# Second layer's experts: outputs added to rows on the chip by one-hot products instead of scatters to memory

## The chip, the cores and the metric

The kernel runs on one core of a Trainium2 chip. A core has a matrix engine (TensorE, in the profile PE, its weight loads PEld), three engines for elementwise work (VectorE = DVE, ScalarE = ACT, GpSimd = POOL), a queue engine (SyncE = SP) and 16 DMA engines that all queues share. The metric is the device time of one execution in microseconds (us); lower is better.

## The reference, cut to what matters

Two blocks of two layers each are computed in float32. The change concerns the last step of the second block's second layer: 16 experts, each of which takes the 64 tokens (of 512) that it rates highest. Every expert's output is scaled by its rating, added into the rows of its tokens, scaled by a gate `m_lat[5]`, and added to the residual `x`. A row can be chosen by several experts or by none.

```python
vals, idx = lax.top_k(aff.transpose(0, 2, 1), cap)          # cap = 64
xg = jax.vmap(lambda hb, ib: hb[ib])(h, idx)
hid = silu(einsum('becd,edf->becf', xg, w_gate)) * einsum('becd,edf->becf', xg, w_up)
out = einsum('becf,efd->becd', hid, w_down) * vals[..., None]
moe = zeros((t, d)).at[ib.reshape(-1)].add(ob.reshape(-1, d))
x = x + m_lat[5] * moe
```

## The kernel before, in words

`block2` runs two layers. In each, `mixer2` does projections and attention and ends with the residual `x` in SBUF, features on partitions; `ffn` then does routing and experts. The first layer (`need` is true) also has a second stream of 256 context rows, and its sums are read back by `reload`; the second layer has only the 512 rows, and its sums are the kernel's output. `self.acc[0]` is a DRAM tensor in the first layer and the output tensor itself in the second.

Routing (`route`, lines 1537 to 1620) computes the ratings, turns `x` back to rows (line 1575) and writes each row block twice to DRAM through GpSimd's queue: normalized to `normed` (line 1578, from a tile `row`) and raw to `acc` (line 1579, from a tile `in`), where it is the start value of the sums. Then it takes the top 64 of each expert by eight rounds on VectorE (lines 1583 to 1589) and lays token numbers and ratings out as `gi` (128 rows of a pair of experts in one column, for gathers), `si` (for scatters) and `vw` (ratings), and the gate over all partitions.

Experts run in eight pairs q (`experts`, lines 1684 to 1783), 64 rows of each expert side by side on 128 partitions. For a pair, `fetch` gathers 128 rows from `normed` on GpSimd's queue, `inputs` transposes them (line 1678) and modulates them, `gate_up` multiplies with two weight matrices (line 1741), `hidden` makes the activations and transposes them (line 1715), `down` multiplies with the third matrix in two halves of 512 columns (line 1768) and scales by rating and gate (line 1771). Then `scatter` issues two indirect DMAs with addition, one per expert, 64 rows of 4 KB each (line 1788). The order is gate_up(0), gate_up(1), down(0), gate_up(2), down(1), ..., gate_up(7), down(6), down(7). The planner of the framework takes this text order as a priority and may put an instruction that it thinks ready ahead of an earlier one on the same engine; at run time each engine keeps that fixed order.

Weights come in 96 pieces of 1 MB through SP's queue (line 1640), twelve per pair. Each piece goes into one of 14 buffers in turn: 11 tiles `ew` and three that reuse the room of `x` and `cx`. A piece's transfer is issued when its buffer is free. The products of rows with weights are float32 with 64 columns of weights per expert, two experts next to each other in the array (TensorE runs each as two instructions); the projections of the layers before use F32R operands split into a rounded part and the rest (lines 472 to 474).

PSUM has banks by name: `g` and `s` two each, `t` two, `o` and `a` one each; in the second layer's experts `o` and `a` are not used.

Of the kernel before, what the change touches and what calls it, by code (L numbers as in the profile page):

```python
# [20 lines left out]
P = 128  # L21
D = 1024
# [26 lines left out]
def _bc(v):  # L49
    return np.ascontiguousarray(np.broadcast_to(v.reshape(1, -1), (P, v.size)))  # L50
# [40 lines left out]
def _layout(inp):  # L91
# [15 lines left out]
    vec, vec2, c2 = {}, {}, {}  # L107
    _layout2(g, A, vec2, c2)
    c2["id"] = np.eye(P, dtype=np.float32)
    A["const1"], coff = _pack(c)  # L110
    A["const2"], coff2 = _pack(c2)
    for l in range(DEPTH):
# [122 lines left out]
class _K:  # L235
# [1301 lines left out]
    def route(self, l, v, x, nt, cap, state, got):  # L1537
# [30 lines left out]
        wk = self.tl("y", [16, 512])[:, :W]  # L1568
        yield
        for i in range(nt):  # L1570
            raw, row = self.tl("in", [P, D]), self.tl("row", [P, D])
            for s in range(2):
                pq = self.pt("s")
                for k in range(4):
                    ten.transpose(pq[:, k * P:(k + 1) * P], x[:, 4 * s + k, i * P:(i + 1) * P], self.idf)
                act.activation(row[:, s * 512:(s + 1) * 512], pq, AF.Copy, scale=rs[:, i:i + 1])
                act.activation(raw[:, s * 512:(s + 1) * 512], pq, AF.Copy)
            nc.gpsimd.dma_start(self.normed[v][i * P:(i + 1) * P, :], row)
            nc.gpsimd.dma_start(self.acc[v][i * P:(i + 1) * P, :], raw)

        val = self.s1(f"val{v}", [16, cap])
        idx = self.s1(f"idx{v}", [16, cap], U32)
# [25 lines left out]
        vec.tensor_copy(si, pg[:cap, 16:32])  # L1608
        vw = self.s1(f"vw{v}", [P, 8])
        vec.tensor_copy(vw, pg[:, 8:16])  # L1610
        yield

        gate = self.s1(f"gate{v}", [P, D])
# [5 lines left out]
            act.activation(gate[:, s * 512:(s + 1) * 512], pq, AF.Copy)  # L1619
        got[v] = gi, si, vw, gate  # L1620

    def ffn(self, l, x, cx, need, states):
        nc, A = self.nc, self.A
        ten, vec, act = nc.tensor, nc.vector, nc.scalar
        acts = [("gu", 0)] + [a for q in range(1, 8) for a in (("gu", q), ("d", q - 1))] + [("d", 7)]
        pieces = []
        for what, q in acts:
            ee = (2 * q, 2 * q + 1)
            if what == "gu":
                pieces += [A[f"{n}{l}"][2 * e + j] for j in range(2) for n in ("eg", "eu") for e in ee]  # L1630
            else:
                pieces += [A[f"ed{l}"][2 * e + j] for j in range(2) for e in ee]

        spare = [x[:, :4], x[:, 4:], cx.rearrange("p (k h) c -> p k (h c)", h=2)]
        loaded = []

        def fetch():
            n = len(loaded) % (EW + len(spare))
            raw = self.tl("ew", [P, 4, 512]) if n < EW else spare[n - EW]
            nc.sync.dma_start(raw, pieces[len(loaded)].rearrange("p (k c) -> p k c", k=4))  # L1640
            loaded.append(raw)

        nxt = [0]

        def eload():
            if nxt[0] == len(loaded):
                fetch()
            nxt[0] += 1
            return loaded[nxt[0] - 1]

        for _ in range(EW):
            fetch()
        streams = [(0, x, 4, 64)] + ([(1, cx, 2, 32)] if need else [])
        got = {}
        run = [self.route(l, v, xs, nt, cap, states[v], got) for v, xs, nt, cap in streams]
        for _ in range(6):
            for r in run:
                next(r, None)
        self.experts(l, acts, got, eload)
        if need:  # L1660
            self.reload(x, cx)
# [22 lines left out]
    def experts(self, l, acts, got, eload):  # L1684
# [2 lines left out]
        nc = self.nc  # L1687
        ten, vec, act, pool = nc.tensor, nc.vector, nc.scalar, nc.gpsimd
        self.mods = {v: self.mod_cols(l, v, 3, self.v(f"n2{l}")) for v in got}
        two = 1 in got  # L1690
        rows, xg, hid = {}, {}, {}

        def fetch(q):
# [26 lines left out]
        def gate_up(q):  # L1720
# [3 lines left out]
            for j in range(2):  # L1724
# [12 lines left out]
                for ps, wn in ((pg, w[0]), (pu, w[1])):  # L1737
                    for k in range(4):
                        d = 4 * j + k
                        for e in range(2):  # L1740
                            ten.matmul(ps[e * 64:(e + 1) * 64], x0[:, d, e * 64:(e + 1) * 64], wn[e][:, k],  # L1741
                                       start=d == 0, stop=d == 7)
            hidden(q, 0, pg, pu, P)

        def down(q):
# [14 lines left out]
                    vec.scalar_tensor_tensor(y[:64, c], ps[r], val[r, q:q + 1], gate[r, c], OP.mult, OP.mult)  # L1760
                self.scatter(1, y, si, q, 32)
            gi, si, val, gate = got[0]
            y = self.tl("row", [P, D])
            for j in range(2):
                ps = self.pt("s")
                for f in range(4):
                    for e in range(2):
                        ten.matmul(ps[e * 64:(e + 1) * 64], hid[0, q][:, f, e * 64:(e + 1) * 64], w[j][e][:, f],  # L1768
                                   start=f == 0, stop=f == 3)
                c = slice(j * 512, (j + 1) * 512)  # L1770
                vec.scalar_tensor_tensor(y[:, c], ps, val[:, q:q + 1], gate[:, c], OP.mult, OP.mult)
            self.scatter(0, y, si, q, 64)

        fetch(0)
        fetch(1)
        inputs(0)
        for what, q in acts:
# [3 lines left out]
                gate_up(q)  # L1781
            else:
                down(q)

    def scatter(self, v, y, si, q, n):

# [24 lines left out]
    def block2(self, x, cx, rb, dram, out):  # L1811
        self.rs2 = self.one("rs2", [P, 6])
        for l in range(DEPTH):
# [2 lines left out]
                states = self.mixer2(l, x, cx, need, *rb)  # L1816
            self.normed = [dram.tile([n, D], F32, name=f"normed{l}{n}", tag=f"n{n}") for n in ((T, 256) if need else (T,))]
            self.acc = [dram.tile([n, D], F32, name=f"acc{l}{n}", tag=f"a{n}") for n in (T, 256)] if need else [out]
            with self.scope(ew=EW, row=4, **{"in": 4}, xg=4, hid0=2, **({"hid1": 2} if need else {}), t=5, sm=2, s1=1):
                self.ffn(l, x, cx, need, states)  # L1820
            rb = None, self.rs2


# [45 lines left out]
```

## Time and profile before

| what | value |
|---|---|
| median of 3 runs | 3001.3 us (3000.87 to 3002.17) |
| the profiled execution's own time | 3005.11 us |
| its span, first to last instruction | 3003.3 us |
| PE busy | 2790.8 us (93%) |
| DVE, ACT, POOL busy | 52%, 40%, 9% |
| mean granted TensorE clock | 0.972 |
| HBM read, written | 416.40 MB, 20.97 MB |
| GB/s in the last four fortieths of the span | 358, 408, 408, 296 |

Averages over the span say little here: the second layer's experts are the last 260 us, in which the DMA engines are at 400 GB/s and more, while the rest of the span is mostly TensorE. A prediction has to be read from that stretch. Lines of the trace carry the source line (L1768), the engine, the operation, and the tiles as out<-in.

### The profile page before, as it was taken

How to read it: one execution, taken by the hardware profiler on the slowest of the kernel's cores; microseconds unless marked ns; L12 is line 12 of the kernel's file. 1: busy time of each engine (PE TensorE's matmuls, PEld its weight loads, DVE VectorE, ACT ScalarE, POOL GpSimd, SP SyncE). 2: the span in 40 equal slices, each digit the busy share in tenths (PEclk: the TensorE clock that was granted, in tenths of full speed). 3: DMA queues.
4: the chain of work that ended last, by engine and by line, in shares of the span. 5: the costliest groups of instructions: out<-in, count | busy, mean ns of one | idle time of the engine just before them, and what ended most of it. 6: DMA issues, size and time to landing. Idle time of an engine off the chain costs nothing. (4 is left out here: it accounts for less than half of the span.)

```text
span 3003.3 us, 46941 instructions
## 1 busy us (share of the span) xinstructions
PE 2790.8 (93%) x19056; PEld 1938.7 (65%) x19056; DVE 1548.1 (52%) x3135; ACT 1198.9 (40%) x2468; POOL 279.7 (9%) x276
## 2 busy tenths in 40 slices
PE   7999999999999999998999999899996999997875
PEld 5677767977677767877776877633324767773321
DVE  4645786545555786645456556711115365574100
ACT  5545354443545354444455243331113363433110
POOL 0000031000000030000011011011111010001101
PEclk9999999999999999998999999999997999998998
DMA  4132425412232434521110111689974111129997
GB/s 141 56 134 92 169 99 175 156 57 79 67 121 92 153 107 142 168 85 52 43 39 22 58 44 30 254 338 373 366 271 132 51 34 56 52 77 358 408 408 296
DMA packets 97576, 439.55 MB, mean 146 GB/s; under 512 B 11216, under 2 KB 12496, under 8 KB 72784
## 3 DMA queue, kind: packets, MB, share of 16 engines
q1 hardware_dynamic: 86976, 401.09, 36.5%
q0 software_dynamic: 9520, 32.32, 4.0%
q8 instruction: 150, 2.46, 0.3%
q10 hardware_dynamic: 864, 3.15, 0.3%
q14 instruction: 66, 0.54, 0.1%
HBM read 416.40 MB, written 20.97 MB: 146 GB/s over the span
## 5 line engine op out<-in xcount | busy, mean ns | idle before, releaser
L472 PE MATMUL psg<-h,wh 128*128 128x512 f32 x1616 | 655.8, 407 | 6.7 <-ACT h L444 4.3
L473 PE MATMUL psg<-h,wh 128*128 128x512 f32 x1616 | 651.3, 403 | 0.0
L474 PE MATMUL psg<-h,wl 128*128 128x512 f32 x1616 | 647.2, 401 | 0.0
L462 DVE TENSOR_TENSOR wl<-wr,wh 128x1024 fp32r<-128x1024 f32 (+2 forms) x272 | 340.1, 1251 | 367.4 <-ACT wh L460 361.4
L460 ACT ACTIVATE wh<-wr 128x1024 fp32r<-128x1024 f32 (+2 forms) x272 | 280.5, 1032 | 470.7 <-PE psg L473 398.1
L472 PEld LDWEIGHTS psg<-h,wh 128*128 128x128 f32 x1616 | 307.5, 190 | 90.1 <-issue 18.5
L473 PEld LDWEIGHTS psg<-h,wh 128*128 128x128 f32 x1616 | 307.9, 191 | 68.6 <-issue 9.7
L474 PEld LDWEIGHTS psg<-h,wl 128*128 128x128 f32 x1616 | 307.2, 190 | 67.8 <-issue 6.0
L1741 PE MATMUL psg<-ew,xg 128*64 128x512 f32 x832 | 223.0, 609 | 22.6 <-DMA ew<-in_eu_dram 11.6
L472 PE MATMUL psg<-y,wh 128*128 128x256 f32 (+1 forms) x560 | 182.2, 326 | 1.5 <-ACT y L448 0.8
L473 PE MATMUL psg<-y,wh 128*128 128x256 f32 (+1 forms) x560 | 180.5, 323 | 1.9 <-DVE y L449 1.9
L474 PE MATMUL psg<-y,wl 128*128 128x256 f32 (+1 forms) x560 | 179.7, 322 | 0.2 <-DVE wl L462 0.2
L1741 PEld LDWEIGHTS psg<-ew,xg 128*64 128x64 f32 x832 | 65.4, 139 | 154.9 <-issue 113.6
L472 PE MATMUL psg<-f,wh 128*128 128x256 f32 (+1 forms) x360 | 113.3, 316 | 7.1 <-DVE x L582 4.9
L472 PEld LDWEIGHTS psg<-y,wh 128*128 128x128 f32 x560 | 108.4, 194 | 15.4 <-issue 2.1
L473 PEld LDWEIGHTS psg<-y,wh 128*128 128x128 f32 x560 | 108.2, 194 | 11.3 <-DVE y L449 2.2
L473 PE MATMUL psg<-f,wh 128*128 128x256 f32 (+1 forms) x360 | 113.0, 314 | 0.8 <-DVE f L1256 0.8
L474 PE MATMUL psg<-f,wl 128*128 128x256 f32 (+1 forms) x360 | 112.4, 312 | 0.6 <-DVE wl L462 0.5
L474 PEld LDWEIGHTS psg<-y,wl 128*128 128x128 f32 x560 | 108.6, 195 | 6.4 <-DVE wl L462 0.5
L1021 ACT ACTIVATE t<-pst 128x512 f32<-128x512 f32 (+1 forms) x134 | 69.4, 556 | 106.4 <-PE pst L1018 106.4
L1768 PE MATMUL pss<-ew,hid 128*64 128x512 f32 x400 | 106.4, 598 | 4.8 <-DMA ew<-in_ed_dram 4.7
L1018 PE MATMUL pst<-const_sb,t 128*128 128x128 f32 x488 | 83.4, 282 | 5.2 <-DVE t L1246 3.5
(484 smaller groups left out, 4583.0 us busy)
## 6 DMA issues: line engine op xcount, KB each, us to landing
ew<-in_eg_dram SPq DMA_DIRECT2D x52, 1024.0 KB, 10.9
ew<-in_eu_dram SPq DMA_DIRECT2D x52, 1024.0 KB, 20.4
ew<-in_ed_dram SPq DMA_DIRECT2D x50, 1024.0 KB, 10.4
wm<-in_wm_dram SPq DMA_DIRECT2D x96, 512.0 KB, 4.3
wr<-in_w_f_dram SPq DMA_DIRECT2D x92, 512.0 KB, 3.5
wr<-in_v_f_dram SPq DMA_DIRECT2D x60, 512.0 KB, 3.2
wr<-in_w_o_dram SPq DMA_DIRECT2D x32, 512.0 KB, 3.5
x<-in_ed_dram SPq DMA_DIRECT2D x10, 1024.0 KB, 16.0
```

The lines of the kernel that those rows point to most:

```text
L460: nc.scalar.activation(hi, raw, AF.Copy)
L462: nc.vector.tensor_tensor(lo, raw, hi, OP.subtract)
L472: t.matmul(ps, a[0], b[0], start=first, stop=False)
L473: t.matmul(ps, a[0], b[1], start=False, stop=False)
L474: t.matmul(ps, a[1], b[0], start=False, stop=last)
L1018: ten.transpose(pp[:, (2 * i + a) * P:(2 * i + a + 1) * P], ps[a][:, c:c + P], self.idf)
L1021: self.nc.scalar.activation(pT[:, :w], pp[:, :w], AF.Copy)
L1741: ten.matmul(ps[e * 64:(e + 1) * 64], x0[:, d, e * 64:(e + 1) * 64], wn[e][:, k], start=d == 0, stop=d == 7)
L1768: ten.matmul(ps[e * 64:(e + 1) * 64], hid[0, q][:, f, e * 64:(e + 1) * 64], w[j][e][:, f], start=f == 0, stop=f == 3)
```

## The change

In the second layer only, the raw rows stay in SBUF as four tiles `sum`, 128 rows of 1024 values each. For every pair a one-hot tile `oh` is made (128 chosen rows by 512 tokens: 1 where the token's number is the row's slot). The scaled output of each half is split into a rounded part (ScalarE) and the rest (VectorE), and for each of the four row blocks two F32R products (rounded part, rest) with a 128x128 slice of `oh` put the rows in their places in a PSUM bank, `o` or `a` in turn; VectorE adds the bank to the tile `sum`. A pair has two halves, four blocks and two products each: 16 products and 8 additions. They are a generator, `add`; the `gate_up` that follows in the order above (after down(0) that of pair 2) takes a step of it, two blocks, after each quarter of a weight piece, and the next `down` takes what is left. For the last pair the finished blocks are written to the output from SP's and ScalarE's queues. The raw rows are no longer written at the start and nothing is scattered. To make room, the layer has 10 tiles `ew` instead of 11, 3 each of `row`, `in` and `xg` instead of 4. A constant `iota` (numbers 0 to 511) is loaded on ScalarE's queue.

```diff
@@ route
-            raw, row = self.tl("in", [P, D]), self.tl("row", [P, D])
+            raw, row = self.tl("in" if self.two else "sum", [P, D]), self.tl("row", [P, D])
...
-            nc.gpsimd.dma_start(self.acc[v][i * P:(i + 1) * P, :], raw)
+            if self.two:
+                nc.gpsimd.dma_start(self.acc[v][i * P:(i + 1) * P, :], raw)
+            else:
+                self.total.append(raw)
...
+        if not self.two:
+            self.slot = self.s1("slot", [P, 8])
+            vec.tensor_copy(self.slot, pg[:, :8])
@@ ffn
-            n = len(loaded) % (EW + len(spare))
-            raw = self.tl("ew", [P, 4, 512]) if n < EW else spare[n - EW]
+            n = len(loaded) % (ew + len(spare))
+            raw = self.tl("ew", [P, 4, 512]) if n < ew else spare[n - ew]
...
+        self.two, self.total = need, []
@@ experts, gate_up
                             ten.matmul(ps[e * 64:(e + 1) * 64], x0[:, d, e * 64:(e + 1) * 64], wn[e][:, k],
                                        start=d == 0, stop=d == 7)
+                    next(spread[0], None)
@@ experts, down
-            y = self.tl("row", [P, D])
+            if two:
+                y = self.tl("row", [P, D])
+            else:
+                for _ in spread[0]:
+                    pass
+                oh = self.tl("oh", [P, 512], F32R)
+                vec.tensor_scalar(oh, io, self.slot[:, q:q + 1], None, OP.is_equal)
+                parts = []
...
-                vec.scalar_tensor_tensor(y[:, c], ps, val[:, q:q + 1], gate[:, c], OP.mult, OP.mult)
-            self.scatter(0, y, si, q, 64)
+                yc = y[:, c] if two else self.tl("t", [P, 512])
+                vec.scalar_tensor_tensor(yc, ps, val[:, q:q + 1], gate[:, c], OP.mult, OP.mult)
+                if not two:
+                    hi, lo = self.tl("yh", [P, 512], F32R), self.tl("yl", [P, 512], F32R)
+                    act.activation(hi, yc, AF.Copy)
+                    vec.tensor_tensor(lo, yc, hi, OP.subtract)
+                    parts.append((hi, lo))
+            if two:
+                self.scatter(0, y, si, q, 64)
+            else:
+                spread[0] = add(q, oh, parts)
+
+        def add(q, oh, parts):
+            for j, y in enumerate(parts):
+                c = slice(j * 512, (j + 1) * 512)
+                for i in range(4):
+                    ps = self.pt("oa"[i % 2])
+                    for n in range(2):
+                        ten.matmul(ps, oh[:, i * P:(i + 1) * P], y[n], start=n == 0, stop=n == 1)
+                    o = self.total[i][:, c]
+                    vec.tensor_tensor(o, o, ps, OP.add)
+                    if q == 7:
+                        (nc.sync, nc.scalar)[i % 2].dma_start(self.acc[0][i * P:(i + 1) * P, c], o)
+                    if i % 2:
+                        yield
+
+        spread = [iter(())]
+        if not two:
+            io = self.tl("y", [P, 512])
+            nc.scalar.dma_start(io, self.A["iota"])
...
+        for _ in spread[0]:
+            pass
@@ block2
-            with self.scope(ew=EW, row=4, **{"in": 4}, xg=4, hid0=2, **({"hid1": 2} if need else {}), t=5, sm=2, s1=1):
+            ew = EW if need else EW - 1
+            more = {"row": 4, "in": 4, "hid1": 2} if need else {"row": 3, "in": 3, "sum": 4, "oh": 1, "yh": 2, "yl": 2}
+            with self.scope(ew=ew, xg=4 if need else 3, hid0=2, **more, t=5, sm=2, s1=1):
```

## Rows read from the trace of the kernel before

**Rows 1.** Busy time by stretch: length, each engine's busy us, PEclk, DMA share, GB/s.

```profile
2742.00:2757.00 15.00, 11.39 (x52) 6.23 (x54) 0.31 (x3) 7.10 (x18) 5.75 (x6) 0.65 0.55 182
2757.00:2822.00 65.00, 62.52 (x298) 22.22 (x296) 7.12 (x10) 12.17 (x30) 6.25 (x5) 1.00 1.00 406
2822.00:2982.00 160.00, 123.84 (x524) 40.18 (x518) 15.13 (x21) 14.34 (x34) 14.03 (x10) 0.98 1.01 404
```

**Rows 2.** Order of time, SP's queue, weight pieces: start, us, engine, line, transfer.

```profile
2756.51 1.17 SPq L1640 DMA_DIRECT2D ew<-in_eu_dram  x2
...
2811.41 0.33 SPq L1640 DMA_DIRECT2D x<-in_eu_dram  x1
2813.90 0.33 SPq L1640 DMA_DIRECT2D x<-in_ed_dram  x1
```

**Rows 3.** DMA queues from 2757 to 2982: packets, MB, share of 16 engines.

```profile
q1 hardware_dynamic: 11808, 85.99, 91.3%
q0 software_dynamic: 1460, 4.96, 9.6%
```

**Rows 4.** Order of time at the end: last products, last scatter.

```profile
2982.30 0.64 PE L1768 MATMUL pss<-x,hid 128*64 128x512 f32 x1 [1.53 <-DMA x<-in_ed_dram]
...
2984.92 1.02 PE L1768 MATMUL pss<-x,hid 128*64 128x512 f32 x2
...
2993.62 1.41 POOL L1788 DMA_INDIRECT out_dram<-row,si  x1 [3.36 <-DMA out_dram<-row,si]
```

**Rows 5.** The closing line's drains: ns min/median/max, first and last start.

```profile
L1864 POOLq DRAIN  x3: 46/102/9153, 2993.4 to 3003.1; - x3
L1864 SPq DRAIN  x3: 7/7/7, 2998.6 to 3002.8; - x3
```

**Rows 6.** Order of time, F32R products of a projection and a weight load.

```profile
2699.10 0.40 PE L474 MATMUL psg<-h,wl 128*128 128x512 f32 x1
2699.10 0.19 PEld L472 LDWEIGHTS psg<-h,wh 128*128 128x128 f32 x1
2699.33 0.40 PE L472 MATMUL psg<-h,wh 128*128 128x512 f32 x1
```

**Rows 7.** Order of time on TensorE, 2753 to 2818, pairs 0 to 2.

```profile
2753.79 1.08 PE L1741 MATMUL psg<-ew,xg 128*64 128x512 f32 x4
...
2783.59 0.59 PE L1768 MATMUL pss<-ew,hid 128*64 128x512 f32 x1
2785.04 0.63 PE L1715 MATMUL pst<-const_sb,t 128*128 128x128 f32 x4 [0.86 <-DVE t L1712]
2785.60 7.08 PE L1768 MATMUL pss<-ew,hid 128*64 128x512 f32 x30
...
2793.64 7.51 PE L1741 MATMUL psg<-ew,xg 128*64 128x512 f32 x33
...
2816.95 0.59 PE L1768 MATMUL pss<-ew,hid 128*64 128x512 f32 x1
```

**Rows 8.** Groups by form: count, busy us, mean ns, idle before, releaser.

```profile
L1771 DVE SCALAR_TENSOR_TENSOR row<-pss,vw,gate 128x512 f32<-128x512 f32 x16 | 12.0, 751 | 67.9 <-PE pss L1768 67.9
...
L545 DVE TENSOR_TENSOR h<-f,h 128x512 fp32r<-128x512 f32 x1 | 0.7, 682 | 0.0
...
L544 ACT ACTIVATE h<-f 128x512 fp32r<-128x512 f32 x1 | 0.6, 633 | 0.8 <-DVE f L1504 0.8
```

**Rows 9.** DMA issues from 2640 to 2694: count, KB, median us to landing.

```profile
wr<-in_v_o_dram SPq DMA_DIRECT2D x4, 256.0 KB, 2.7
```

**Rows 10.** Line 1578, the writes of normed: landing.

```profile
DMA to landing us min/median/max: 5.4/8.7/12.0
```

**Rows 11.** Order of time in routing: write of normed, fourth row, first gather.

```profile
2723.32 0.62 POOL L1578 DMA_DIRECT2D normed<-row  x1 [58.63 <-ACT row L1576]
...
2728.36 0.72 ACT L1576 ACTIVATE row<-pss,rq_y 128x512 f32<-128x512 f32 x1
...
2743.76 1.02 POOL L1666 DMA_INDIRECT in<-normed,gi  x1 [12.09 <-DVE vw L1610]
```

More of the change, by code (lines that the diff above doesn't have):

```diff
@@ L109, in _layout @@
     c2["id"] = np.eye(P, dtype=np.float32)
+    A["iota"] = _bc(np.arange(T, dtype=np.float32))
     A["const1"], coff = _pack(c)
@@ L1620, in route, with ffn @@
         got[v] = gi, si, vw, gate
-    def ffn(self, l, x, cx, need, states):
+    def ffn(self, l, x, cx, need, states, ew):
         nc, A = self.nc, self.A
@@ L1649, in eload @@
             return loaded[nxt[0] - 1]
-        for _ in range(EW):
+        for _ in range(ew):
             fetch()
         streams = [(0, x, 4, 64)] + ([(1, cx, 2, 32)] if need else [])
+        self.two, self.total = need, []
         got = {}
@@ L1689, in experts @@
         self.mods = {v: self.mod_cols(l, v, 3, self.v(f"n2{l}")) for v in got}
-        two = 1 in got
+        two = self.two
         rows, xg, hid = {}, {}, {}
@@ L1818, in block2 @@
             self.acc = [dram.tile([n, D], F32, name=f"acc{l}{n}", tag=f"a{n}") for n in (T, 256)] if need else [out]
-            with self.scope(ew=EW, row=4, **{"in": 4}, xg=4, hid0=2, **({"hid1": 2} if need else {}), t=5, sm=2, s1=1):
-                self.ffn(l, x, cx, need, states)
+            ew = EW if need else EW - 1
+            more = {"row": 4, "in": 4, "hid1": 2} if need else {"row": 3, "in": 3, "sum": 4, "oh": 1, "yh": 2, "yl": 2}
+            with self.scope(ew=ew, xg=4 if need else 3, hid0=2, **more, t=5, sm=2, s1=1):
+                self.ffn(l, x, cx, need, states, ew)
             rb = None, self.rs2
```

## The prediction

> **What bounds the kernel now.** I read in this order: busy time by stretch for the end of the kernel, where layer 2's experts run; then the order of issue on SP's queue; then the table of DMA queues; then TensorE's order of time; last the end. By stretch [rows 1], the weight prefetch has stopped between 2742 and 2757 (DMA share 0.55: every weight buffer is full until the first products free one), and from 2757 to 2982 the 16 DMA engines are busy without a gap (share 1.00 to 1.01, 404 to 406 GB/s), while TensorE has idle time only after 2822. So the stage is bounded by TensorE at first, working off what was prefetched, and by the weight stream afterwards. The reader should see on SP's queue that undisturbed 1 MB pieces are issued 2.49 us apart [rows 2]; that is what the engines can take. The queue table of the same 225 us [rows 3] says who else uses them: 82 pieces on q1 take 91.3% (205.4 us, 2.505 each), the GpSimd queue q0 takes 9.6% (21.6 us). That queue carried 13 scatters and 2 gathers there. The last piece arrives at 2982.30, TensorE ends at 2985.94, and then four scatters, each waiting for the one before, and GpSimd's drain run to 3003.3 [rows 4, 5].
>
> **The change, part by part.** Layer 1 is untouched by every edit (`two` is true there). I work in times of the profiled execution; its span is 3003.3 and its time 3005.1, while the median of the runs is 3001.3, so differences are taken from the profile and subtracted from the median.
>
> *Scatters out of the stream.* 13 of the 16 lie in the stretch of [rows 3]. A gather has the bytes of two plain scatters, 0.52 MB, or 1.25 us at the pace of [rows 2]; two of them leave 21.6 - 2.5 = 19.1 us, 1.47 a scatter. The lower bound is their own 0.26 MB at the weights' pace, 0.62 each, 8.1 in all. I take 19.1, because the row is that queue's own and its share and q1's fill the engines completely. The four initial writes of `raw` (2 MB) go as well, but before 2742, ahead of a gap; worth nothing.
>
> *One weight buffer less.* The stream restarts when gate_up(0) frees its first buffers, at 2756.5 [rows 2], with 83 pieces to go and not 82: +2.5 us. Together: the last piece lands at 2982.3 - 19.1 + 2.5 = 2965.7, and with its 3.64 us of products [rows 4] the **DMA line** ends at 2969.4 (2980.4 with the lower bound).
>
> *One-hot products on TensorE.* Per pair 4 row blocks x 2 halves x 2 passes = 16 products of 128x512 in F32R. The nearest row is the projection's F32R product of the same size, 0.23 apart [rows 6]: 3.73 us. They come in four groups of four between the 64-column products; a switch there and back costs about 0.2 (four 64-column products take 1.08 between two groups of transposes; 33 in a run take 7.51, so four 0.91) [rows 7]: 0.9 for four groups. So **a = 4.6 us a pair**; below 3.7 nothing reaches, the upper end stands under the rivals. TensorE now needs 23.3 us from the start of gate_up(2) to the last product of down(1), with no weight missing [rows 7]; from 2793.6, six such pairs and 7.0 for down(7), as down(0) takes there, end at 2940.4. Seven additions (pairs 0 to 6) stand before the end: the **TensorE line** is 2940.4 + 7a = 2972.6. Each microsecond of a costs seven.
>
> So the two lines almost meet: as the stream gets faster, TensorE is late next. The additions of pair 6 are drained ahead of down(7). VectorE paces them: the chain from a half's last product is the gated scaling 0.75, ScalarE's rounding 0.63, the difference 0.68 [rows 8], about 2.3 with hops; then 8 additions of about 0.75 (a two-operand read of PSUM, as L1771 [rows 8]). That is 8.3 against 4.6 already counted, so 0 to 3.7 more; I take 2. TensorE ends at 2974.6, not 2985.9.
>
> *The end.* Of pair 7: scaling, rounding, difference 2.3; then 8 additions at 0.72 to 0.75, one of which fits into ScalarE's step: 8.0 in all after the last product (7.3 to 9). The last of eight writes of 256 KB: a 256 KB load on SP's queue lands in 2.7, a 512 KB write on the loaded GpSimd queue in 5.4 at least [rows 9, 10]; I take 2.7 + 0.3 for the issue, since nothing else is under way by then. SP has seen today's last scatter by 2998.6 and starts its drain, yet GpSimd's, 9.15 us long, holds the end until 3002.5 [rows 5]. With no scatter GpSimd is done long before; what is left is 0.75 from there to 3003.3, the closing barrier, and some 0.5 for SP's own last waits: 1.3. The end is 12.3 after the last product (11 to 16) against 17.4 now.
>
> *Edits that cost nothing while their cover holds.* Two roundings, two differences, the one-hot and 8 additions put some 8 us a pair on VectorE and 1.3 on ScalarE; by stretch VectorE is busy 15 of 160 us and ScalarE 14 [rows 1]. The iota load and the copy of `slot` stand behind the routing values and are needed first in down(0). The two banks of the additions are unused in this layer. Without that cover TensorE waits, which is a. `row` shrinks to 3 buffers: ScalarE's fourth `row` (2728.36) then waits for the first write of `normed` (issued 2723.32, landing 5.4 to 12.0 later) [rows 10, 11], 0.4 to 7 us, and behind it wait the gate's activations and the last write of `normed`, on which the first gather (2743.76) depends; that write would land at 2736.4 to 2749.6, so the gather is delayed by 0 to 5.8. I take 0: the `raw` writes that shared the queue are gone.
>
> **Sum.** 2974.6 + 12.3 = 2986.9 of span, 16.4 less than 3003.3; the median goes to 2984.9.
>
> **Rivals.** (1) *TensorE takes the bound's place.* If at two of a pair's four groups the product must wait out one addition on VectorE (0.75), a = 6.1, and TensorE ends at 2983.1 + 2: 2995.4 for the median. For it: with one bank each, a block's products need the addition two blocks earlier to be done. Against: between groups lie two 64-column products of a piece's quarter, 0.85, longer than an addition. (2) *Additions stand bare, slower.* The order on TensorE isn't the text's: down's first two products stand ahead of the transposes of the hidden rows, which then wait 0.86 on VectorE [rows 7]. If each half's additions are placed straight behind its products, TensorE waits out the chain twice: 2.3 + two additions 1.5 + products and hops 0.7 = 4.5 a half, a = 9.0, an end at 3003.4 + 12.3: 3013.7. It decides from a = 7.2, where 2940.4 + 7a + 12.3 passes 3003.3. Against: `next(spread[0])` stands inside gate_up's loop, behind work that is ready. (3) *Weight loads come bare.* If each of the 16 products had to wait for its 0.19 us load [rows 6], a = 7.6: 2993.6 + 2 + 12.3, or 3005.9. Against: loads of that size lie between products 0.23 apart [rows 6], so here they are hidden. The Trainium skill (TensorE: Matmul & The Clock Gate, Part 3, "What overlaps and what doesn't") says that a weight load overlaps running products only where their row groups differ, which for full-height operands would make it bare; [rows 6] disagree, so it gets little. (4) *Better*: a near 3.7, additions of pair 6 hidden, a tail of 11: 2969.4 + 11, or 2978.4.
>
> [...]
>
> **How the numbers follow.** Forecast 0.65 (2979 to 2991); rival 1 0.13 (2991 to 3000); rival 2 0.10; rival 3 0.05; rival 4 0.07. The likeliest gives 2985. 2977 to 2998 takes in the forecast, most of rival 1 and half of rival 4, some 8 in 10. About 0.2% (6 us) is what a measurement can tell from no change: faster 0.79 (forecast, rival 4, half of rival 1), same 0.11 (rival 3, the other half), slower 0.10.
>
> **What would show it.** Right: from 2757 pieces 2.5 us apart throughout and q0 near 1%; TensorE's idle time after 2822 nearly gone and down(7) ending near 2975; F32R products about 0.23 apart; no long drain of GpSimd. Wrong: waits of TensorE for VectorE's sums totalling over 15 us (rivals 1, 2); F32R products 0.4 apart (rival 3); pieces still 2.75 apart on average; a first gather after 2744.

## The result and the profile after

The changed kernel takes 3021.2 us (median of 6 runs, 3017.0 to 3024.2) against 3001.5 for the kernel before on the same chip: a ratio of 1.0064 [1.0052, 1.0077], slower by 0.64%. The prediction said 2985, between 2977 and 2998. It was wrong in sign.

The profiled execution took 3021.7 us, with a span of 3019.9. Its busy time by stretch, as in [rows 1] (length, PE, PEld, DVE, ACT and POOL busy with their instructions, granted clock, DMA share, GB/s):

```profile
2742.00:2757.00 15.00, 15.00 (x64) 5.01 (x65) 0.00 (x0) 6.10 (x17) 1.88 (x2) 0.91 0.68 240
2757.00:2822.00 65.00, 60.86 (x263) 21.82 (x259) 15.94 (x24) 13.35 (x33) 2.81 (x3) 0.97 1.01 421
2822.00:2982.00 160.00, 148.27 (x579) 51.10 (x580) 45.58 (x70) 20.01 (x43) 0.00 (x0) 0.96 0.90 370
```

Before, the last stretch had the DMA engines full at 1.01 and TensorE busy for 124 of 160 us [rows 1]. Now the DMA share is 0.90 and TensorE is busy for 148: the bound has changed places. The queue table of 2757 to 2982 (packets, MB, share of 16 engines), which answers to [rows 3], shows that the scatters are gone; GpSimd's q0 carries little but the gathers:

```profile
q1 hardware_dynamic: 11650, 84.79, 91.6%
q0 software_dynamic: 432, 1.57, 1.7%
```

TensorE waits for no weight in this stage. What it waits for is new (waits of TensorE from 2757 to 3020: us in total, times, longest):

```profile
PE pso L1806 <- ACT yh L1791: 11.7, 8, 1.9
PE pso L1806 <- DVE sum L1808: 6.9, 13, 0.6
PE pst L1723 <- DVE t L1720: 1.7, 2, 0.9
```

L1806 is the one-hot product, L1791 ScalarE's rounding of a half, L1808 VectorE's addition into the sum. TensorE's order of time in one pair, the changed kernel, second layer of pair 2 and first matrices of pair 4 (L1784 is `down`, L1749 is `gate_up`; start, us, engine, line, tiles, count, wait):

```profile
2843.76 3.65 PE L1784 MATMUL pss<-ew,hid 128*64 128x512 f32 x16
2848.97 0.50 PE L1806 MATMUL pso<-yh,oh 128*128 128x512 f32 x1 [1.56 <-ACT yh L1791]
2849.31 0.40 PE L1806 MATMUL psa<-yh,oh 128*128 128x512 f32 x1
2849.70 0.50 PE L1806 MATMUL pso<-yl,oh 128*128 128x512 f32 x1
2850.04 0.40 PE L1806 MATMUL psa<-yl,oh 128*128 128x512 f32 x1
2850.98 0.80 PE L1806 MATMUL pso<-yh,oh 128*128 128x512 f32 x1 [0.55 <-DVE sum L1808]
2851.57 0.63 PE L1806 MATMUL pso<-yl,oh 128*128 128x512 f32 x1
2852.13 4.55 PE L1784 MATMUL pss<-ew,hid 128*64 128x512 f32 x14
...
2857.28 1.07 PE L1749 MATMUL psg<-ew,xg 128*64 128x512 f32 x2
2858.28 0.50 PE L1806 MATMUL pso<-yh,oh 128*128 128x512 f32 x1
...
2860.25 0.50 PE L1806 MATMUL pso<-yh,oh 128*128 128x512 f32 x1 [0.55 <-DVE sum L1808]
2860.69 3.65 PE L1749 MATMUL psg<-ew,xg 128*64 128x512 f32 x14
```

This is where the time went, and the reader should see three things. First, the place: the additions of a pair's first half stand in the middle of that pair's own second layer (14 records of L1784 still follow), so TensorE waits 1.56 us for VectorE's scaling and ScalarE's rounding of the half that it has just finished. The text puts them into the next `gate_up`. Second, groups come behind a single product of the first expert, torn off from its neighbour: the two records of L1749 at 2857.28 stand alone. Third, the 14 records of L1784 behind the wait take 4.55 us where 14 of L1749 take 3.65; from 2850 to 2854 the granted clock has a mean of 0.57, so it is at the lower of its two levels (1.2 and 2.4 GHz) for most of these 4 us. By stretch again, the third column from the end being the granted clock:

```profile
2846.00:2850.00 4.00, 2.44 (x11) 0.84 (x8) 1.44 (x2) 0.63 (x1) 0.00 (x0) 1.00 1.02 430
2850.00:2854.00 4.00, 3.45 (x10) 1.13 (x10) 1.97 (x3) 0.00 (x0) 0.00 (x0) 0.57 1.02 430
```

To compare stages I use one landmark, the transposes of a pair's hidden rows (L1723; L1715 before), and the end of the span. These are its rows in the changed kernel for pairs 1, 2 and 7:

```profile
2777.23 0.63 PE L1723 MATMUL pst<-const_sb,t 128*128 128x128 f32 x4 [0.87 <-DVE t L1720]
2806.86 0.66 PE L1723 MATMUL pst<-const_sb,t 128*128 128x128 f32 x4
...
2979.43 0.66 PE L1723 MATMUL pst<-const_sb,t 128*128 128x128 f32 x4
```

Pair 1 to 2 is a stretch without missing weights (29.63 us here), pairs 2 to 7 are five periods (172.57 / 5 = 34.51), and from pair 7 to the end are 40.5. The same for all kernels, each from its own rows and span; each ratio is to runs of the kernel before that were made beside it (medians 3000.3 to 3002.3):

| kernel | median us | ratio to before | pair 1 to 2 | later pairs, each | pair 7 to end | pair 1 to end |
|---|---|---|---|---|---|---|
| before | 3001.5 | | 23.46 | 31.62 | 36.7 | 218.3 |
| changed | 3021.2 | 1.0064 [1.0052, 1.0077] | 29.63 | 34.51 | 40.5 | 242.7 |
| e1_no_add | 2974.9 | 0.9905 [0.9888, 0.9921] | 23.46 | 29.61 | 23.7 | 195.2 |
| b1_ten_buffers | 3004.3 | 1.0004 [0.9995, 1.0014] | 23.46 | 32.17 | 36.4 | 220.7 |
| b2_no_scatter | 2984.0 | 0.9940 [0.9923, 0.9957] | 23.46 | 28.81 | 33.6 | 201.1 |
| e2_pinned | 2999.2 | 0.9989 [0.9980, 0.9999] | 29.64 | 30.41 | 35.9 | 217.6 |
| e3_hi_only | 3008.1 | 1.0020 [1.0010, 1.0029] | 27.53 | 32.34 | 37.9 | 227.1 |
| e5_two_groups | 2983.6 | 0.9946 [0.9929, 0.9962] | 26.62 | 29.13 | 32.6 | 204.8 |
| e4_hi_two_groups | 2983.0 | 0.9942 [0.9925, 0.9958] | 24.79 | 29.32 | 33.3 | 204.7 |
| e6_fp32 | 3009.9 | 1.0031 [1.0019, 1.0044] | 30.49 | 32.28 | 36.2 | 228.1 |
| e7_split | 2989.5 | 0.9963 [0.9949, 0.9977] | 28.92 | 30.06 | 30.7 | 209.9 |
| e8_ready_torn | 3020.1 | 1.0058 [1.0041, 1.0075] | 28.22 | 34.62 | 38.7 | 240.0 |
| e10_pool_ready | 3004.3 | 1.0011 [1.0002, 1.0021] | 29.63 | 32.75 | 31.4 | 224.7 |

The changed kernel loses 6.2 us from pair 1 to 2, 5 x 2.89 = 14.5 in the later pairs and 3.8 at the end, 24.4 in all. The medians differ by only 19.7, because this profile reaches pair 1 at 2777.2 and that of before at 2785.0. The profiles of the kernels made from the changed one reach it between 2776.3 and 2783.0, those of b1 and b2 at 2780.8 and 2785.1. Between before and changed the difference is nearly whole by 2510, ahead of the edited code (the last F32R product on a tile `f` stands at 2516.5 and 2508.8). The profiled execution of before was itself 3.8 us above the median of its runs; what the rest comes from was not looked into, and I give the change nothing for it.

### The profile page after: what moved, and what is told of

Read it like the earlier page. It is cut to its first block, busy times and chain, and to the rows that moved or that the text cites. A ratio compares the mean times of both kernels' runs of the same rounds, so it can differ in the third digit from the quotient of the medians.

```text
span 3019.9 us, 47278 instructions
## 1 busy us (share of the span) xinstructions
PE 2841.4 (94%) x19183; PEld 1957.0 (65%) x19184; DVE 1603.1 (53%) x3224; ACT 1208.8 (40%) x2484; POOL 255.0 (8%) x256
## 5 line engine op out<-in xcount | busy, mean ns | idle before, releaser
L1749 PE MATMUL psg<-ew,xg 128*64 128x512 f32 x808 | 212.9, 600 | 0.1
L1749 PEld LDWEIGHTS psg<-ew,xg 128*64 128x64 f32 x808 | 62.4, 137 | 123.7 <-issue 120.6
L1784 PE MATMUL pss<-ew,hid 128*64 128x512 f32 x408 | 116.9, 639 | 0.0
```

## The experiments

My theory after the result: the stream was freed as predicted, and all that was lost lies in the additions on TensorE. Rivals: taking the scatters out did not free the stream; or the products cost much more than 0.23 us wherever they stand. Only the core of each edit is shown.

**The floor without additions: e1_no_add.**

```diff
-                    hi, lo = self.tl("yh", [P, 512], F32R), self.tl("yl", [P, 512], F32R)
-                    act.activation(hi, yc, AF.Copy)
-                    vec.tensor_tensor(lo, yc, hi, OP.subtract)
-                    parts.append((hi, lo))
+                    parts.append(yc)
...
-                    ps = self.pt("oa"[i % 2])
-                    for n in range(2):
-                        ten.matmul(ps, oh[:, i * P:(i + 1) * P], y[n], start=n == 0, stop=n == 1)
                     o = self.total[i][:, c]
-                    vec.tensor_tensor(o, o, ps, OP.add)
+                    if q == 7 and i == 0:
+                        vec.tensor_tensor(o, o, y, OP.add)
```

> The changed kernel without its additions: no rounding, no difference, no one-hot products, no VectorE sums except one at the end for each half; the outputs of all experts but a part of the last pair's are left out of the result. Ten buffers, no scatters. What it measures is the stage without the work that the change adds. Theory (the weights were the bound before, the scatters held the transfer engines for 1.47 us each, and everything that was lost lies in the additions on TensorE): the weights run at 2.5 us a piece without a break, the DMA line of the prediction ends at 2969.4 in the frame of the earlier profile, and with some 10 us behind it the span is 2979, the median 2975 to 2981. TensorE's pair without additions takes 23.3 us against 29.9 for its weights, so it waits for weights again. Rival (taking the scatters out did not free the stream, or ten buffers starve it): 2990 to 3001, with pieces still 2.9 us apart or more.

2974.9, at the lower edge of what the theory expected. TensorE waits for weights again (waits from 2800 to 2950, two of the rows):

```profile
PE psg L1749 <- DMA ew<-in_eu_dram: 9.3, 7, 1.4
PE psg L1749 <- DMA ew<-in_eg_dram: 9.3, 7, 1.3
```

So 46 us lie in the additions of the changed kernel: 3021.2 less 2974.9. The rival on the stream falls.

**What one buffer and the scatters are worth: b1_ten_buffers, b2_no_scatter.** b1 is the kernel before with ten `ew` tiles in the second layer's experts; b2 is

```diff
-        for e in range(2):
+        for e in range(2 if 1 in self.mods or q == 7 else 0):
```

> The kernel before with ten weight buffers in the second layer's experts instead of eleven, nothing else. By the prediction one buffer is worth one piece of run-ahead, 2.5 us: 3004. Rivals: 0 (the stream is bound by the transfers, and the run-ahead is not used up): 3001.5; 7 us or more, if the scatters' pauses can't be made good with a shorter run-ahead: 3009.

> The kernel before, with the scatters of pairs 0 to 6 of the second layer left out (their part of the output is missing); pair 7's two stay, eleven buffers stay, and nothing is added on the chip. It prices the scatters by themselves. By the prediction 13 of them stand in the way of the weights with 1.47 us each: 19.1 us, 2980 to 2984. By the prediction's lower bound, 8.1 us, the scatters mostly fit beside the weights: 2992 to 2995. If they cost nothing beside the weights, 3001.

b1: 3004.3 against 3001.8 for before, +2.6 by the medians and +2.4 from pair 1 to the end, as predicted; the interval of the ratio, -1.5 to +4.2 us, takes in zero. b2: -16.3 by the medians and -17.2 from pair 1 to the end. The products of the last piece, which started at 2982.30 before [rows 4], start at 2968.05 (pair 1 stands at 2785.09 there, 2785.04 before): the 13 scatters in the stream held it up by 14.3 us, 1.1 each and not 1.47. The remaining 3 us came at the end.

**Place alone: e2_pinned.** The additions stay, but the one-hot block gets a factor one that is worked out from weights of the next pair. The planner then can't place them earlier.

```diff
+                if not j:
+                    self.late = w[1][1][:, 0, :1]
...
-                oh = self.tl("oh", [P, 512], F32R)
-                vec.tensor_scalar(oh, io, self.slot[:, q:q + 1], None, OP.is_equal)
...
+            one = self.sm("one", [P, 1])
+            late = last if q == 7 else self.late
+            vec.tensor_tensor(one, late, late, OP.is_equal)
+            oh = self.tl("oh", [P, 512], F32R)
+            vec.tensor_scalar(oh, io, self.slot[:, q:q + 1], one, OP.is_equal, OP.mult)
```

> The changed kernel with all its additions; only the one-hot block is made later: its scale is a one worked out from the weights of the next pair's second matrix, so no addition can stand ahead of that point and all 32 products of a pair's second layer stand together. Theory A (the loss is in where the additions stand: straight behind the products whose result they need, so that TensorE waits for ScalarE and VectorE and its clock falls): the waits of 2.7 us and the half-clock 1.5 us a pair go, what stays is 16 products at 0.24 to 0.33 and four switches at 0.57, so 6 to 7.5 a pair, 23.3 + 6 to 7.5 = 29.3 to 30.8 a pair against 35.2: seven pairs less 31 to 41 us, 2980 to 2992. Theory B (the additions cost TensorE 9 us or more wherever they stand, by the products and the switches themselves): 32.3 us a pair or more, 3001 to 3012. Theory C (the place plays no part): 3021.

2999.2: 22 us are gone with the place, so theory C falls, and B's 32.3 us a pair with it; but it is 7 above the range of theory A. TensorE's waits for the rounding and for the sums fall from 18.6 us in the changed kernel to 1.6 + 2.2 (2757 to the end), and the granted clock is 1.00 throughout from 2757 to 2950. The later pairs, 30.41 each, are as A expected. Pair 1 to 2 is 29.64, as in the changed kernel, where pair 0's additions already stood in `gate_up`. And the pin does not hold pair 6's additions, since no `gate_up` follows; they wait bare once more:

```profile
2968.53 0.50 PE L1810 MATMUL pso<-yh,oh 128*128 128x512 f32 x1 [1.56 <-ACT yh L1791]
...
2970.53 0.80 PE L1810 MATMUL pso<-yh,oh 128*128 128x512 f32 x1 [0.55 <-DVE sum L1812]
```

**Half the products: e3_hi_only.**

```diff
-                    hi, lo = self.tl("yh", [P, 512], F32R), self.tl("yl", [P, 512], F32R)
+                    hi = self.tl("yh", [P, 512], F32R)
                     act.activation(hi, yc, AF.Copy)
-                    vec.tensor_tensor(lo, yc, hi, OP.subtract)
-                    parts.append((hi, lo))
+                    parts.append((hi,))
...
-                    for n in range(2):
-                        ten.matmul(ps, oh[:, i * P:(i + 1) * P], y[n], start=n == 0, stop=n == 1)
+                    ten.matmul(ps, oh[:, i * P:(i + 1) * P], y[0], start=True, stop=True)
```

> The changed kernel with one pass instead of two: the second product of each block, with the rounding error of the outputs, and the VectorE difference that makes it are left out; the planner may still put the additions behind the products they need. Theory A (of 11.9 us a pair, 6.0 are products, and the rest waits, switches and half clock that stay): half the products go, 3.0 us a pair, 7 x 3.0 = 21: 2998 to 3004. Theory B (the products themselves are the cost, 0.6 to 0.7 us each with all that hangs on them): 6 us a pair, 2979 to 2985. If only the 0.23 us of a dense product go: 8 x 0.23 x 7 = 13, 3008.

3008.1, 13.1 below the changed kernel: 7 x 8 x 0.233 = 13.0. From pair 1 to the end it is 15.6 less, 2.2 in each later pair against 8 x 0.233 = 1.9. Leaving out half of the products saves little more than their dense price. Both theories missed, and the third figure was right: most of what hangs on the additions does not go with their number.

**Few groups between whole products: e5_two_groups, e4_hi_two_groups.** The pin moves to the rounding, so that each half has its own; a group has four PSUM banks; pair 6's additions go between the halves of pair 7. e4 leaves out the second pass besides.

```diff
-                    next(spread[0], None)
+                next(spread[0], None)
...
+                    if q == 7:
+                        self.late = w[j][1][:, 0, :1]
+                        next(ahead, None)
...
+                    one = self.sm("one", [P, 1])
+                    vec.tensor_tensor(one, self.late, self.late, OP.is_equal)
+                y = [self.tl("yh", [P, 512], F32R)]
+                act.activation(y[0], yc, AF.Copy, scale=one)
...
-                    ps = self.pt("oa"[i % 2])
+                    ps = self.pt("oass"[i])
```

> All additions in full, but gathered: a pair's 16 one-hot products in two groups of 8 over four PSUM banks, each group between two whole products of the next pair (held there by scaling the rounded half by a one made from that pair's weights), pair 6's between the two halves of pair 7's second layer. Theory A (what an addition costs is its 0.233 us a product and some 0.53 us of each change between the two kinds of product): a = 16 x 0.233 + 2 x 0.53 = 4.8 us a pair, close to the prediction's 4.6; 23.6 + 4.8 = 28.4 us is below the 29.8 us that a pair's weights take, the weights are the bound again until the last two pairs, and the whole comes to 2984 to 2990. Theory B (the number of changes plays no part; with e2_pinned's 2999.2 the products, VectorE's sums or PSUM set the cost): 2996 to 3002.

> As e5_two_groups with one pass: the products of the rounding errors are left out of the sums, so two groups of 4 products a pair. Theory A: a = 8 x 0.233 + 2 x 0.53 = 2.9 us a pair, 26.5 us against 29.8 of weights: TensorE has 3 us to spare in each pair, the additions of pairs 0 to 5 are hidden, and only those of pairs 6 and 7 stand at the end: 2979 to 2984, some 5 below e5_two_groups. Theory B (what is left stands in the end alone, the products' number plays no part): as e5_two_groups within 2 us.

e5: 2983.6, 37.6 below the changed kernel and 0.54% faster than before, with the whole work of the change. It is 0.4 below theory A's range, and theory B falls. One group of e5 in TensorE's order of time, pair 1's additions between the first and the second half of `gate_up(3)`:

```profile
2811.54 7.04 PE L1750 MATMUL psg<-ew,xg 128*64 128x512 f32 x32
2818.51 0.50 PE L1814 MATMUL pso<-yh,oh 128*128 128x512 f32 x1
2818.84 0.39 PE L1814 MATMUL pso<-yl,oh 128*128 128x512 f32 x1
2819.07 0.39 PE L1814 MATMUL psa<-yh,oh 128*128 128x512 f32 x1
...
2820.23 0.39 PE L1814 MATMUL pss<-yl,oh 128*128 128x512 f32 x1
2820.55 3.65 PE L1750 MATMUL psg<-x,xg 128*64 128x512 f32 x16
```

Behind the first, the products of the group are 0.23 apart, and none waits. The last record of L1750 ahead of it starts at 2811.54 + 7.04 - 0.59 = 2817.99, and the next would follow 0.213 later, at 2818.20; it comes at 2820.55. The group costs 2.35 us, 8 x 0.233 and 0.49 for going to the other kind of product and back. Two groups a pair make 4.7. Now TensorE waits for weights again (waits from 2757 to 2950):

```profile
PE psg L1750 <- DMA ew<-in_eu_dram: 4.9, 4, 1.3
PE pst L1723 <- DVE t L1720: 1.7, 2, 0.9
PE psg L1750 <- DMA ew<-in_eg_dram: 0.6, 1, 0.6
```

e4: 2983.0 lies in theory A's range, but it is no better than e5, where A had some 5 us less; by that it is B's figure. Where no weight is missing, its second pass shows (24.79 and 26.62 from pair 1 to 2, 1.83 = 8 x 0.229); in the later pairs the weights take 29 us anyway, and the end did not get shorter.

**A group torn up: e7_split.** One line of e5 changes: the condition is a weight piece of the first matrix.

```diff
-                self.late = w[1][1][:, 0, :1]
+                self.late = w[0][1][:, 0, :1]
```

> As e5_two_groups, with one weight piece earlier as the condition: the planner now puts each group of 8 products around one product of the next matrix (3, one fp32 product of the first expert, 5, then the seven others), so that the products of the two experts, which otherwise run side by side, are torn apart there. Seen in the stretch from the hidden transposes of pair 1 to those of pair 2, where no weight is awaited: 23.46 us without additions, 26.62 in e5_two_groups. Theory A (tearing a pair of products costs one more half, 0.43 us, beside 0.4 to 0.5 us for one more change between kinds): 26.62 + 2 x 0.9 = 28.4. Theory B (only changes between kinds cost): 27.5. Theory C (neither costs): 26.6. The whole stays near e5_two_groups, since 28.4 is still below the 29.8 us of a pair's weights: 2983 to 2989.

The whole, 2989.5, is 5.9 above e5 and just outside what I expected. The stretch that I had named doesn't serve: from pair 1 to 2 the planner tore only one group, and 28.92 is above all three figures. In `gate_up(5)` both groups are torn. One of them:

```profile
2881.05 0.40 PE L1814 MATMUL psa<-yh,oh 128*128 128x512 f32 x1
2881.38 1.07 PE L1750 MATMUL psg<-ew,xg 128*64 128x512 f32 x2
2882.38 0.50 PE L1814 MATMUL psa<-yl,oh 128*128 128x512 f32 x1
```

The next addition would have started at 2881.28 and starts at 2882.38. So the lone product and the change there and back take 1.10 us. Beside its neighbour it would have taken 0.43, and a change costs 0.49: some 0.2 are left here, and more where the other expert's product comes back alone. That is theory A in kind; the price of the tear by itself is not measured more closely than that.

**Another kind of product: e6_fp32.**

```diff
-                oh = self.tl("oh", [P, 512], F32R)
+            oh = self.tl("oh", [P, 512])
...
-                    for n in range(2):
-                        ten.matmul(ps, oh[:, i * P:(i + 1) * P], y[n], start=n == 0, stop=n == 1)
+                    ten.matmul(ps, oh[:, i * P:(i + 1) * P], y, start=True, stop=True)
```

> As e2_pinned, with plain fp32 one-hot products: one product a block and 0.853 us each (two records of 0.427 us in the unchanged part of the profile), no rounding, no difference, and no change between kinds of product. Theory A (in e2_pinned each of five changes a pair costs 0.53 us): a = 8 x 0.853 = 6.8 us against 16 x 0.233 + 5 x 0.53 = 6.4: the same as e2_pinned within 4 us, 2996 to 3003. Theory B (changes between the kinds cost nothing): 8 x (0.853 - 0.466) = 3.1 us a pair more than e2_pinned, 3017 to 3024.

3009.9, between the two. The blocks cost more than the 0.853 that I had taken, and one product between two of them costs as much as a block:

```profile
2855.97 1.13 PE L1806 MATMUL pso<-yh,oh 128*128 128x512 f32 x2
2856.93 1.02 PE L1806 MATMUL psa<-yh,oh 128*128 128x512 f32 x2
2857.88 2.79 PE L1751 MATMUL psg<-ew,xg 128*64 128x512 f32 x10
...
2868.01 1.07 PE L1751 MATMUL psg<-x,xg 128*64 128x512 f32 x2
2869.02 1.13 PE L1806 MATMUL pso<-yh,oh 128*128 128x512 f32 x2
```

Two blocks take 1.91, or 0.955 each: 7.6 a pair and not 6.8. The lone product at 2868.01 holds TensorE for 1.01 us, although here no kind of product changes. So the tear has a price of its own, about 0.6 us (1.01 less the 0.43 beside a neighbour). The two prices do not add up, though: tear and change together took 1.10 in e7, the tear without a change 1.01 here, a change without a tear 0.49 in e5. Theory B's free change doesn't fit either: the dense F32R products with free changes would be 3.9 a pair below e6 (7.6 less 3.7), but e2 is only 1.9 below in the later pairs.

**The wait alone: e8_ready_torn, e10_pool_ready.** Both keep two banks and the changed kernel's groups behind torn-off products, and are meant to take away only the wait for a half just made; to that end the additions move into the next pair's first matrices. e8 is e5 with `self.late = w[0][0][:, 0, :1]` and banks `"oa"[i % 2]`; in e10 the halves are rounded at once and only the one-hot block is late, by GpSimd:

```diff
+                oh = self.tl("row", [P, D])[:, :512]
+                vec.tensor_scalar(oh, io, self.slot[:, q:q + 1], None, OP.is_equal)
...
+            pool.tensor_tensor(one, late, late, OP.subtract)
+            oh = self.tl("oh", [P, 512], F32R)
+            pool.tensor_scalar(oh, oh0, one, None, OP.add)
```

> All additions in full, with the changed kernel's own pattern (groups of 5 and 6 straight behind one torn-off product, the rest behind the seven others, two PSUM banks), but moved into the next pair's first matrices, where the rounded halves and differences have long been made: the condition is the first weight piece of each half. What it leaves out against the changed kernel is only the wait for the chain of a half just computed, and the low clock behind that wait; changes between kinds of product, torn products and waits for VectorE's sums stay. The changed kernel needs 34.5 us a pair in the steady part. Theory A (the bare chain, some 1.6 to 1.9 us a pair, and the half clock behind it, some 1.6, are less than half of the 11 us; changes, tears and waits for sums are the rest): 31 to 33 us a pair, 3000 to 3012. Theory B (the bare chain and the clock are most of it): 30 us a pair or less, 2986 to 2996. The clock should stay at its full level in both.

> Once more the changed kernel's pattern on TensorE without the wait for a fresh half; in e8_ready_torn that wait had come back through VectorE's queue (1.72 us behind the scaling of the other half). Now the rounded halves and differences are made at once, and only the one-hot block goes through GpSimd, which is idle here, with a zero worked out from the next pair's first weight piece added to it. Groups of 7, 2 and 7 products a pair, straight behind a torn-off product or seven whole ones, two PSUM banks. What goes against the changed kernel is the wait of 1.6 to 1.9 us a pair for ScalarE's rounding and the low clock behind it (some 1.6 us); changes of kind, torn products and waits for VectorE's sums stay. Theory A (these three are more than half of the 11 us a pair): 31 to 32.5 us a pair in the steady part instead of 34.5, 3000 to 3010. Theory B (the wait for the chain and the clock are most of it): 30.3 us or less, as in e7_split, 2987 to 2996. Clock at its full level from 2822 to 2950 in both.

e8 failed as an experiment: 3020.1, because the wait was back (first row). VectorE's tiny operation and the rounding stand in their queues behind the scaling of the other half, which TensorE has only just finished. In e10 that wait is gone, and VectorE's queue shows up in the sums instead (second row):

```profile
2851.84 0.50 PE L1814 MATMUL pso<-yh,oh 128*128 128x512 f32 x1 [1.72 <-ACT yh L1808]
```

```profile
2854.24 0.50 PE L1812 MATMUL pso<-yh,oh 128*128 128x512 f32 x1 [1.75 <-DVE sum L1814]
```

e10 takes 3004.3, inside theory A's range: without the wait for a fresh half, and in the other place, 17 us go, and from there to e5, with whole groups and four banks, another 21. A's steady pair (31 to 32.5) was missed slightly, at 32.75, since the waits for sums grew from 6.9 to 11.9 us; and the clock did not stay full as both theories had it, its mean from 2822 to 2950 is 0.96, in e8 too. So neither prices the wait by itself.

## Why the prediction was wrong

**The step that failed: where the additions stand.** The sum took them in four groups between `gate_up`'s products, behind work that is ready, because the text has them there. On TensorE the additions of a half stand straight behind its products, from pair 1 on. The trace of before had shown that TensorE's order isn't the text's [rows 7]; the prediction quoted that, as rival 2, and set it aside with the place in the text. It should have carried most of the weight. What it looks like from the runs: pair 0's additions stand in `gate_up(2)`, where the weights had been fetched ahead, and pair 1's and later ones stand at points where the next product needs a piece of its own. That the planner reckons with weights still missing there, and fills the gap with additions, fits this, but it is argued; that the place costs 22 us is shown by e2. The other 14 of the 36 us between 2985 and 3021.2 were missing even with the place as the sum had it (pair 6's additions aside), most of them in a second term, a.

**Rival 2 was right in kind and too small.** It had a = 9.0 and 3013.7, with a chance of 0.10. From the table a is 34.51 - 23.46 = 11.05 in the later pairs. In the pair shown, TensorE waits 1.56 + 0.55 + 0.55 = 2.7 us. The mark that the prediction set for rivals 1 and 2, over 15 us of waits for VectorE's sums, is not reached by its letter (6.9); with the waits for ScalarE's rounding it is 11.7 + 6.9 = 18.6. What the rival left out are the torn products and the lower clock behind the waits; there the first two F32R products are 0.59 apart (2850.98 to 2851.57), where they are 0.34 apart at the full clock (2848.97 to 2849.31).

**The size of a, where the place is right.** The sum had a = 4.6 for four groups. In the changed kernel pair 0's additions stand in `gate_up(2)` as the text has them, and there a is 29.63 - 23.46 = 6.2; in e2's later pairs it is 30.41 - 23.46 = 6.95. Over seven pairs that is 11 to 16 us. The products were right (0.233), but a change there and back is 0.49 and not 0.225, so that four groups come to 3.7 + 4 x 0.49 = 5.7; what is left goes with groups that are torn. Two whole groups cost 4.7 in e5, and that this is close to the sum's 4.6 is luck. The row that the price came from has products and transposes of one kind [rows 7]; it holds no change between F32R and float32 at all, and should have been a bound from below.

**The stream.** The scatters were worth 14.3 us in the stream, 1.1 each, and not 19.1: that term was a third too big. With the end they were worth 16.3 to 17.2. The reason that I gave, q0's share in [rows 3], counts the time of its packets; part of it presumably lay beside other packets, which no run shows by itself. One buffer is 2.4 to 2.6, as predicted. In e1 the products of the last piece start at 2966.0, that is 2971.9 in the frame of before (pair 1 5.9 later there); the sum had 2965.7.

**The end.** From the last product of `down(7)` to the end: 3019.9 - 3010.1 = 9.8 in the changed kernel and some 13.4 in e5, against 12.3 predicted. The last writes landed 2.1 us after their issue (median, on either queue) and not 2.7. The prediction counted four scatters behind TensorE's end; with 13 of 16 in the stream there are three, issued at 2983.45, 2988.87 and 2993.62, and the first of them before TensorE ended. The sum took the end of before from its rows, so nothing hangs on that. GpSimd's long drain is no longer at the end: its rows have a first start of 2809.0.

```profile
L1912 POOLq DRAIN  x3: 46/97/12262, 2809.0 to 3019.6; - x3
```

**Costs put at nothing.** The first gather is issued at 2735.96, 7.8 us earlier than before [rows 11], and pair 1 is earlier by as much, so the third `row` buffer costs nothing that shows. VectorE and ScalarE have time enough by the stretch, 46 and 20 of 160 us, but that says nothing of their queues: e8 and e10 show TensorE waiting 1.7 us for an instruction that stands behind another half's scaling.

**Rival 1** (waits for sums at two of four groups) is there, with 6.9 us in all, as the smaller part. What was set against it, 0.85 us between groups, misreads the code: a step of `add` comes after eight products, all that one matrix has with half of the features, and not after a quarter of a weight piece, as the words on the change have it too. In the changed kernel pair 0's first three groups start at

```profile
2789.41 0.50 PE L1806 MATMUL pso<-yh,oh 128*128 128x512 f32 x1
...
2794.12 0.50 PE L1806 MATMUL pso<-yh,oh 128*128 128x512 f32 x1
...
2798.83 0.50 PE L1806 MATMUL pso<-yh,oh 128*128 128x512 f32 x1
```

which leaves some 3.6 us between them, and none of them waits. The cover was better than the prediction had it, as long as the additions stood there.

**Rival 3** falls: in e5's group 128-column weights are loaded, 0.19 us each, for products 0.23 apart. The rule of the Trainium skill (TensorE: Matmul & The Clock Gate, Part 3, "What overlaps and what doesn't") that was weighed there doesn't hold for these products.

**The prediction's place, enforced**, is e2, with four groups a pair, one of them torn, behind work that is ready: 2999.2, and that is outside the range too. e5 comes to the predicted time by another arrangement, two whole groups of eight with four banks: 204.8 us from pair 1 to the end where the sum had 2986.9 - 2785.0 = 201.9, and 2983.6 for the median where it had 2985. That the medians agree so closely is partly luck, since e5's profile reaches pair 1 8.7 us earlier than that of before. So the change can save what was predicted of it, but not as it is written, nor by its place alone.

## What to carry to other kernels

Where a planner orders an engine, the place of new work in the text is a wish: price it at the worst place that its inputs allow, times the number of rounds, and, if that decides, tie it to something that arrives when its cover does. Put work of another kind into few groups with a bank for each result, and between whole sets of products that run side by side. When a bound is lifted and the next one is within a few per cent, the forecast hangs on the second: a microsecond a round was worth seven here.

## What the hardware showed that was not expected

Two 64-column products of the two experts run at the same time: in e5 their records start together and the next two follow 0.43 later. So a product torn off from its neighbour takes its own time alone (1.01 us in e6). The Trainium skill (TensorE: Matmul & The Clock Gate, Part 3, "Packing small matmuls — row/col tiling") has matmuls in different parts of the array run concurrently; these rows agree.

```profile
2824.04 0.59 PE L1750 MATMUL psg<-cx,xg 128*64 128x512 f32 x1
2824.04 0.59 PE L1750 MATMUL psg<-ew,xg 128*64 128x512 f32 x1
2824.47 0.59 PE L1750 MATMUL psg<-cx,xg 128*64 128x512 f32 x1
```

The clock: in the changed kernel its mean from 2850 to 2854 is 0.57, behind a wait of 1.56 us and one of 0.55 with single products between them; in e2 and e5, where TensorE has no such waits from 2757 to 2950, it is 1.00 throughout, though e5 waits up to 1.3 us for weights. But in e8 it stays at 1.00 from 2850 to 2866, with a wait of 1.72 us and two of some 0.55 in it, and falls in a later pair (0.50 from 2889 to 2893). What tells these apart stays open.
